# A two-layer trunk on one core: where the first loads are queued, where eight low parts are subtracted, and who writes the indexer's key a second time

## The chip, the core and the metric

The kernel runs on one core of one Trainium2 chip. The core has five engines, each with a queue of its own that it works through in order: TensorE (PE: matmuls, and PEld for the loads of their weights), VectorE (DVE), ScalarE (ACT), GpSimd (POOL) and SyncE (SP), which here only issues DMAs. 16 DMA engines move data between the chip's memory (HBM) and the core's SBUF. The metric is the device time of one execution in microseconds (us); a profile shows one execution.

## The reference

The trunk has two layers on 256 tokens of width 1024. Layer 0 is a sparse attention whose keys are chosen by an indexer, layer 1 a stick-breaking attention; each has a SiLU gate, an output projection and a layer norm of ALPHA * x + sublayer(x). What matters here is layer 0:

```python
q, k, v, g, qi, wi, ki = jnp.split(x @ w_in, cuts, axis=-1)
q = apply_rope(q.reshape(b, s, N_HEADS, HEAD_DIM), cos, sin)
k = apply_rope(k.reshape(b, s, N_HEADS, HEAD_DIM), cos, sin)
qi = apply_rope(qi.reshape(b, s, IDX_HEADS, IDX_DIM), cos, sin)
ki = apply_rope(ki[:, :, None, :], cos, sin)[:, :, 0, :]
...
rel = jax.nn.relu(jnp.einsum('bqhd,bsd->bqhs', qib, ki).astype(jnp.float32) * IDX_DIM ** -0.5)
score = jnp.einsum('bqhs,bqh->bqs', rel, wib)
...
_, idx = lax.top_k(score, k_top)
```

The 16 heads then attend to the 64 chosen keys (softmax), and `(o * silu(g)) @ w_out` goes into the layer norm. All is float32.

## The kernel before, in words

**Two parts for each number.** Every matmul of a projection works on a pair: a high part `wh` (the weight rounded to TensorE's float32r format, by ScalarE, L66) and a low part `wl` (the weight less its high part, by VectorE, L67). Three products are added: high by high, low activation by high weight, high activation by low weight. So one chunk is read by 8 matmuls of its `wh` and then by 4 of its `wl` (`tok_part`, L118); in the gates by 8 and 8 (L150, L152).

**Chunks.** All weights of both layers stand in HBM as 80 chunks of 128 x 1024 numbers, 512 KB each, in the order in which they are read. Layer 0's are q0 (chunks 0 to 3), k0 (4 to 7), v0 (8 to 11), k1 (12 to 15), q1 (16 to 19), v1 (20 to 23), eight gates (24 to 31) and the output projection (32 to 39). `fetch` loads a chunk into one of 4 `raw` buffers, through SP's queue, and splits it into one of 8 pairs of `wh` and `wl`. `load_chunk` keeps a few chunks ahead.

**The start.** Before the chunks come eight K tiles (`x_idx`): for each eighth of the width, 128 rows of the transposed x and of the indexer's weights, 420 KB. The first is loaded in three pieces; tiles 1 and 3 are issued from ScalarE's queue (L171), the others from SP's (L79). They take the same `raw` and `wh`/`wl` buffers. TensorE multiplies them in order (L231) into four banks `psi`.

**The indexer.** `rope` (L212 to L221) makes two products on VectorE (`ra`, `rb`) and adds them. For each of the two tiles of 128 tokens it is called for heads 0 to 4 and for heads 5 to 7 with the key, which is head 8; then GpSimd copies the key from place 8 to place 9 (L241), so that one transpose of places 8 and 9 (L275) gives the key twice, one copy for each half of the partitions. From the transposes come `zh`, `zl` (the key's parts) and `qih`, `qil` (L252, L253, in `select`), then scores (`rel` on ScalarE, `sc` on VectorE) and the choice of 64 keys by eight rounds of maximum and replacement for each token tile (L304, L305).

**Order.** `mix` interleaves the projections q0, k0, v0 with `select`; then a loop over the heads runs k1, q1, v1, the gates and the output projection beside the attention. On each engine a scheduler sets the order from this program, and the pools' free buffers set waits. Three banks (`pp`) hold projections: a block needs two, one for each token tile, so that k1's second token tile (L118) waits until ScalarE has copied v0's first tile out (`vt`, L357), and q1's second one until VectorE's rope of k1 has read its bank (`rb`, L219).

Of the kernel before, what the change touches and what calls it, by code (L numbers as in the profile page):

```python
# [9 lines left out]
F32 = mybir.dt.float32  # L10
F32R = mybir.dt.float32r
AF = mybir.ActivationFunctionType
OP = mybir.AluOpType

P = 128
# [5 lines left out]
HD = 64  # L21
# [7 lines left out]
CW = 1024  # L29
WARM = 6  # L30
AHEAD = 2
IDX_A = 5 * HD
IDX_W = IH * HD + HD + IH
NEG_ADM = -1.0e38
# [8 lines left out]
def trunk(ctx: ExitStack, tc: tile.TileContext, x_rows, x_idx, w_all, consts, lnp, out):  # L43
    nc = tc.nc

    def pool(name, bufs, **kw):
        return ctx.enter_context(tc.tile_pool(name=name, bufs=bufs, **kw))
# [5 lines left out]
    wraw = pool("wraw", 4)  # L53
    wspl = pool("wspl", 8)
# [5 lines left out]
    def as32(t):  # L60
        return t.bitcast(F32)
# [3 lines left out]
    def split(h, lo, src):  # L65
        copy = nc.scalar.activation(h, src, AF.Copy)  # L66
        nc.vector.tensor_sub(lo, src, as32(h))  # L67
        return copy
# [8 lines left out]
    def load(dst, src):  # L77

        tc.keep_in_program_order(nc.sync.dma_start(dst, src))  # L79

    ahead = []
    n_chunk = [0]

    def fetch():
        c = n_chunk[0]
        if c == w_all.shape[0]:
            return
        n_chunk[0] += 1
        raw = wraw.tile([P, CW], F32, name="raw", tag="raw")
        load(raw, w_all[c])  # L90
        wh = wspl.tile([P, CW], F32R, name="wh", tag="wh")
        wl = wspl.tile([P, CW], F32R, name="wl", tag="wl")
        split(wh, wl, raw)
        ahead.append((wh, wl))

    def load_chunk():
        while len(ahead) <= AHEAD:
            n = len(ahead)
            fetch()
            if len(ahead) == n:  # L100
                break
        return ahead.pop(0)

    def bank(p, w=512):
        return p.tile([P, 512], F32, name="bank", tag="bank")[:, :w]
# [59 lines left out]

    cuts = (slice(0, IDX_A), slice(IDX_A, IDX_W))
    idx_w = []
    for k in range(KT):
        raw = wraw.tile([P, CW], F32, name="raw", tag="raw")[:, :S + IDX_W]
        if k:  # L170
            (nc.scalar.dma_start if k in (1, 3) else load)(raw, x_idx[k])  # L171
        else:
            first = S + IDX_A
            load(raw[:, :S], x_idx[k, :, :S])
            nc.scalar.dma_start(raw[:, S:first], x_idx[k, :, S:first])
            load(raw[:, first:], x_idx[k, :, first:])
        wh = wspl.tile([P, CW], F32R, name="wh", tag="wh")[:, :IDX_W]
        wl = wspl.tile([P, CW], F32R, name="wl", tag="wl")[:, :IDX_W]
        if k:
            split(xTh[:, k], xTl[:, k], raw[:, :S])  # L180
        else:
            nc.vector.tensor_copy(xTh[:, k], raw[:, :S])
            nc.vector.tensor_sub(xTl[:, k], raw[:, :S], as32(xTh[:, k]))
        for c in cuts if k == 0 else (slice(0, IDX_W),):
            copy = split(wh[:, c], wl[:, c], raw[:, S + c.start:S + c.stop])
            if k == 0:
                tc.keep_in_program_order(copy)
        idx_w.append((wh, wl))

    fetch()  # L190
    cs = cst.tile([P, C_W], F32, name="cs")
    load(cs, consts)
# [18 lines left out]
        nc.gpsimd.memset(as32(zl), 0.0)  # L211
        zpad.append((zh, zl))  # L212

    def rope(dst, ps, heads, t):
        v = ps.rearrange("p (h d) -> p h d", d=HD)
        a = wk.tile([P, 8, HD], F32, name="ra", tag="ra")[:, :heads]
        b = wk.tile([P, 8, HD], F32, name="rb", tag="rb")[:, :heads]
        nc.vector.tensor_mul(a, v, cos[:, t, None, :].to_broadcast([P, heads, HD]))
        nc.vector.tensor_mul(b, v, sin[:, t, None, :].to_broadcast([P, heads, HD]))  # L219
        halves = [u.rearrange("p h (e d) -> p h e d", e=2) for u in (dst, a, b)]  # L220
        nc.vector.tensor_add(halves[0], halves[1], halves[2][:, :, ::-1, :])  # L221


    psi = [[bank(at) for _ in range(2)] for t in range(NT)]
    for k in range(KT):
        w = idx_w[k]
        for xp, wp in ((0, 0), (1, 0), (0, 1)):
            xk = (xTh, xTl)[xp]
            for t in range(NT):
                for n in range(2):  # L230
                    nc.tensor.matmul(psi[t][n][:, :cuts[n].stop - cuts[n].start],  # L231
                                     xk[:, k, t * P:(t + 1) * P], w[wp][:, cuts[n]],
                                     start=k + xp + wp == 0, stop=k == 7 and wp == 1)
    for _ in range(AHEAD):
        fetch()
    ri, wi = [], []
    for t in range(NT):
        r = sb.tile([P, D], F32, name=f"ri{t}", tag=f"x{t}")[:, :10 * HD].rearrange("p (h d) -> p h d", d=HD)
        rope(r[:, :5], psi[t][0][:, :IDX_A], 5, t)
        rope(r[:, 5:9], psi[t][1][:, :4 * HD], 4, t)  # L240
        nc.gpsimd.tensor_copy(r[:, 9], r[:, 8])  # L241
        w = few.tile([P, IH], F32, name=f"wi{t}")
        nc.vector.tensor_scalar(w, psi[t][1][:, 4 * HD:4 * HD + IH], float(np.float32(IH ** -0.5)), None,
                                op0=OP.mult)
        ri.append(r)
        wi.append(w)
# [304 lines left out]
    for t in range(NT):  # L551
        for n in range(2):
            if t == 0:
                wv[n] = list(load_block())
            ps = bank(pp)
# [160 lines left out]
```

## Time and profile before

| | |
|---|---|
| median of 3 runs | 309.99 us (309.28 to 310.41) |
| the profiled execution | 310.33 us, of which the span from the first to the last instruction is 308.4 us |
| TensorE busy | 296.5 us (96%) |
| VectorE, ScalarE, GpSimd busy | 245.1, 203.7, 9.0 us |
| chain that ended last | 83% TensorE, 7% VectorE, 5% DMA |
| read from HBM | 49.05 MB |

A busy TensorE includes matmuls that overlap their neighbours, so its share says when it stood, not how well it ran. Times in the rows below count from the start of the span. A row of the timeline gives start, duration, engine, line, operation, what is written from what, shapes and count; in brackets stands how long the engine was idle before and what ended that.

### The profile page before, as it was taken

What the parts mean: (1) busy time and instruction counts of PE and PEld (TensorE: products, weight loads), DVE (VectorE), ACT (ScalarE), POOL (GpSimd) and SP (SyncE); (2) the same over time, 40 slices, a digit from 0 to 9 for tenths busy, and PEclk for the clock granted to TensorE, in tenths of its full rate; (3) what the DMA queues carried; (4) which work ended last, traced back from release to release, by engine and by line L of the source; (5) the groups of instructions that cost most, each with busy time, mean ns of one, the idle gap of its engine ahead of it and who ended that gap; (6) DMA issues with size and microseconds to landing.
All of it is one profiled execution on the core that took longest, in us unless ns stands there. A gap on an engine that the chain in (4) does not pass through costs nothing.

```text
span 308.4 us, 4668 instructions
## 1 busy us (share of the span) xinstructions
PE 296.5 (96%) x1640; PEld 248.7 (81%) x1640; DVE 245.1 (79%) x517; ACT 203.7 (66%) x427; POOL 9.0 (3%) x18
## 2 busy tenths in 40 slices
PE   7998999999999999999999999999999999999990
PEld 4886888787888888878788888888888888877790
DVE  3669999899999687977499573886898999884385
ACT  4656673475569999998415374767599999985200
POOL 3011000000000000000010100000000000000011
PEclk9999999999999999999999999999999999999997
DMA  7796543876068854254424459785543353000003
GB/s 262 229 349 189 177 156 112 275 258 218 9 240 270 307 191 140 105 216 134 166 68 132 142 154 385 251 292 167 190 132 88 118 160 115 0 2 1 0 16 122
DMA packets 14567, 50.40 MB, mean 163 GB/s; under 512 B 1616, under 2 KB 2000, under 8 KB 14544
## 3 DMA queue, kind: packets, MB, share of 16 engines
q1 hardware_dynamic: 14112, 49.08, 48.5%
q10 hardware_dynamic: 432, 1.02, 0.9%
q8 instruction: 13, 0.21, 0.3%
q14 instruction: 10, 0.08, 0.1%
HBM read 49.05 MB, written 1.05 MB: 162 GB/s over the span
## 4 chain that ended last, share of the span: by engine, by line
PE 83%; DVE 7%; DMA 5%; ACT 1%; issue 1%; POOL 0%; DVEq 0%; SPq 0%; ACTq 0%
PE bank L118 36%; PE bank L150 19%; PE bank L152 10%; PE bank L372 3%; DVE wl L67 3%; DMA raw<-x_idx 3%; DMA raw<-w_all 2%; PE bank L141 1%; PE bank L373 1%; PE bank L605 1%; PE bank L142 1%; PE bank L143 1%; ACT wh L66 1%; DVE sc L305 1%; PE bank L584 1%
## 5 line engine op out<-in xcount | busy, mean ns | idle before, releaser
L66 ACT ACTIVATE wh<-raw 128x1024 fp32r<-128x1024 f32 (+2 forms) x89 | 90.0, 1017 | 52.0 <-DMA raw<-w_all 30.8
L67 DVE TENSOR_TENSOR wl<-raw,wh 128x1024 fp32r<-128x1024 f32 (+2 forms) x89 | 103.5, 1166 | 25.3 <-ACT wh L66 24.9
L118 PE MATMUL bank<-wh,xT 128*128 128x512 f32 x192 | 49.8, 395 | 1.4 <-ACT vt L357 0.7
L150 PE MATMUL bank<-yT,wh 128*128 128x512 f32 x192 | 48.6, 395 | 0.0
L118 PEld LDWEIGHTS bank<-wh,xT 128*128 128x128 f32 x192 | 35.3, 188 | 9.4 <-ACT vt L357 1.2
L150 PEld LDWEIGHTS bank<-yT,wh 128*128 128x128 f32 x192 | 34.5, 188 | 7.1 <-issue 0.3
L152 PEld LDWEIGHTS bank<-yT,wl 128*128 128x128 f32 x192 | 26.2, 190 | 1.9
L152 PE MATMUL bank<-yT,wl 128*128 128x256 f32 x192 | 26.7, 282 | 0.0
L118 PE MATMUL bank<-wl,xT 128*128 128x512 f32 x96 | 26.7, 390 | 0.0
L118 PEld LDWEIGHTS bank<-wl,xT 128*128 128x128 f32 x96 | 18.0, 188 | 3.9
L118 PE MATMUL bank<-wh,oh 128*128 128x512 f32 (+1 forms) x80 | 20.8, 355 | 0.0
L118 PE MATMUL bank<-wh,ol 128*128 128x512 f32 (+1 forms) x80 | 20.7, 350 | 0.0
L118 PE MATMUL bank<-wl,oh 128*128 128x512 f32 (+1 forms) x80 | 20.3, 349 | 0.0
L118 PE MATMUL bank<-wh,yT 128*128 128x512 f32 x64 | 17.4, 391 | 0.0
L150 PE MATMUL bank<-xT,wh 128*128 128x512 f32 x64 | 16.3, 396 | 0.0
L118 PEld LDWEIGHTS bank<-wh,ol 128*128 128x128 f32 x80 | 14.0, 189 | 2.1 <-issue 0.2
L118 PEld LDWEIGHTS bank<-wl,oh 128*128 128x128 f32 x80 | 14.0, 189 | 2.0 <-issue 0.2
L118 PEld LDWEIGHTS bank<-wh,oh 128*128 128x128 f32 x80 | 13.5, 189 | 2.3 <-issue 0.6
L428 ACT ACTIVATE p<-ml,mx 128x128 f32<-128x128 f32 (+1 forms) x32 | 14.2, 448 | 1.2 <-DVE mx L423 1.1
L155 DVE TENSOR_TENSOR bank<-bank,low 128x256 f32<-128x256 f32 x32 | 13.6, 424 | 0.7 <-ACT low L154 0.4
L118 PEld LDWEIGHTS bank<-wh,yT 128*128 128x128 f32 x64 | 11.9, 188 | 2.4
L150 PEld LDWEIGHTS bank<-xT,wh 128*128 128x128 f32 x64 | 11.7, 188 | 2.3
(138 smaller groups left out, 508.1 us busy)
## 6 DMA issues: line engine op xcount, KB each, us to landing
raw<-w_all SPq DMA_DIRECT2D x80, 512.0 KB, 4.2
raw<-x_idx SPq DMA_DIRECT2D x5, 420.0 KB, 4.2
gb<-lnp SPq DMA_DIRECT2D x4, 512.0 KB, 6.2
x<-x_rows SPq DMA_DIRECT2D x2, 512.0 KB, 4.4
y<-x SPq DMA_DIRECT2D x4, 256.0 KB, 2.0
raw<-x_idx ACTq DMA_DIRECT2D x2, 420.0 KB, 5.2
cs<-consts SPq DMA_DIRECT2D x1, 512.0 KB, 6.8
raw<-x_idx ACTq DMA_DIRECT2D x1, 160.0 KB, 2.7
```

The lines of the kernel that those rows point to most:

```text
L66: copy = nc.scalar.activation(h, src, AF.Copy)
L67: nc.vector.tensor_sub(lo, src, as32(h))
L118: nc.tensor.matmul(ps, src[kk][xp][:, t * P:(t + 1) * P], wc[wp][:, k, :], start=kk == 0 and xp + wp == 0, stop=kk == 7 and wp == 1)
L141: nc.tensor.matmul(ps, sh, mh, start=first, stop=False)
L142: nc.tensor.matmul(ps, sh, ml, start=False, stop=False)
L143: nc.tensor.matmul(ps, sl, mh, start=False, stop=last)
L150: nc.tensor.matmul(ps, wh[:, k, :], both[:, k], start=k == 0, stop=k == 7)
L152: nc.tensor.matmul(ps[:, :S], wl[:, k, :], high[:, k], start=False, stop=k == 7, skip_group_check=True)
L155: nc.vector.tensor_add(ps[:, :S], ps[:, :S], low)
L305: nc.vector.match_replace(out=sc, in_to_replace=m8, in_values=sc, imm_value=NEG_REP)
L372: nc.tensor.matmul(po[rs, n * S:(n + 1) * S], vt[0][:, hs], p0(i), start=True, stop=False)
L428: nc.scalar.activation(p[:, i, :], m[:, i, :], AF.Exp, bias=mx[:, c], scale=-1.0, accum_out=sm[:, c])
```

## The change

Three things change. All eight K tiles are issued from SP's queue, except the middle piece of the first. The indexer's key is written to places 8 and 9 by `rope` itself: its last add is split into one for the other heads and one that writes the key twice. And for chunks 6, 9, 12, 15, 18, 21, 24 and 27 (`DMA_LOW`), ScalarE writes the negated high part into `wl` and the high part into `wh`, and a DMA issued by GpSimd adds the chunk from HBM to `wl`, in place of VectorE's subtraction. Those chunks are begun up to two places earlier than they are read (`begin`), which also changes the order of SP's loads: 4, 6, 5, 7, 9, 8, 10, 12, 11 and so on.

```diff
+DMA_LOW = range(6, 30, 3)
...
+    begun = {}
+
+    def begin(c):
+        raw = wraw.tile([P, CW], F32, name="raw", tag="raw")
+        load(raw, w_all[c])
+        wh = wspl.tile([P, CW], F32R, name="wh", tag="wh")
+        wl = wspl.tile([P, CW], F32R, name="wl", tag="wl")
+        if c in DMA_LOW:
+            nc.scalar.activation(wl, raw, AF.Copy, scale=-1.0)
+            nc.scalar.activation(wh, raw, AF.Copy)
+            nc.gpsimd.dma_start(wl, w_all[c], accum_op=OP.add)
+        else:
+            split(wh, wl, raw)
+        begun[c] = wh, wl
...
-        raw = wraw.tile([P, CW], F32, name="raw", tag="raw")
-        load(raw, w_all[c])
-        wh = wspl.tile([P, CW], F32R, name="wh", tag="wh")
-        wl = wspl.tile([P, CW], F32R, name="wl", tag="wl")
-        split(wh, wl, raw)
-        ahead.append((wh, wl))
+        for n in range(c, c + 3):
+            if n not in begun and (n == c or n in DMA_LOW):
+                begin(n)
+        ahead.append(begun.pop(c))
...
-            (nc.scalar.dma_start if k in (1, 3) else load)(raw, x_idx[k])
+            load(raw, x_idx[k])
...
-        nc.vector.tensor_add(halves[0], halves[1], halves[2][:, :, ::-1, :])
+        one = heads - twice
+        nc.vector.tensor_add(halves[0][:, :one], halves[1][:, :one], halves[2][:, :one, ::-1, :])
+        if twice:
+            last = [u[:, one:].to_broadcast([P, 2, 2, HD // 2]) for u in (halves[1], halves[2][:, :, ::-1, :])]
+            nc.vector.tensor_add(halves[0][:, one:], *last)
...
-        rope(r[:, 5:9], psi[t][1][:, :4 * HD], 4, t)
-        nc.gpsimd.tensor_copy(r[:, 9], r[:, 8])
+        rope(r[:, 5:10], psi[t][1][:, :4 * HD], 4, t, twice=True)
```

The order of instructions moves with it. The names are the program's, with their buffers' numbers; line numbers differ between the two, since the changed kernel is 20 lines longer.

First place: ScalarE's row about the key's high part `zh0`, before (chunks 4, 5 and 6 stand ahead of it)

```order
L66 ACTIVATE wh_384<-raw_382 128x1024
L66 ACTIVATE wh_402<-raw_400 128x1024
L66 ACTIVATE wh_491<-raw_489 128x1024
L252 ACTIVATE zh0_177<-bank_406 64x256
L252 ACTIVATE qih_325<-bank_413 128x512
```

and now (chunk 4, then 6 with L95 and L94 about chunk 5).

```order
L68 ACTIVATE wh_384<-raw_382 128x1024
L95 ACTIVATE wh_390<-raw_388 128x1024
L68 ACTIVATE wh_409<-raw_407 128x1024
L94 ACTIVATE wl_391<-raw_388 128x1024
L272 ACTIVATE zh0_177<-bank_413 64x256
L272 ACTIVATE qih_325<-bank_420 128x512
```

One activation of 1024 columns more stands ahead of `zh0`, and chunk 5 comes after chunk 6.

Second place: VectorE's row up to k0's rope (`ra`, `rb`), before (the low part is that of chunk 9; three others stand between `zl` and this one)

```order
L67 TENSOR_TENSOR wl_578<-raw_575,wh_577 128x1024
L297 SCALAR_TENSOR_TENSOR sc0_469<-rel_585,wi0_309,sc0_469 128x128
L297 SCALAR_TENSOR_TENSOR sc1_470<-rel_593,wi1_323,sc1_470 128x256
L297 SCALAR_TENSOR_TENSOR sc0_469<-rel_585,wi0_309,sc0_469 128x128
L297 SCALAR_TENSOR_TENSOR sc1_470<-rel_593,wi1_323,sc1_470 128x256
L218 TENSOR_TENSOR ra_609<-bank_487,cs_167 128x512
```

and now (the low parts are those of chunks 8, 10, 11 and 13; that of 7 stands further ahead).

```order
L69 TENSOR_TENSOR wl_552<-raw_549,wh_551 128x1024
L317 SCALAR_TENSOR_TENSOR sc0_476<-rel_559,wi0_309,sc0_476 128x128
L69 TENSOR_TENSOR wl_632<-raw_629,wh_631 128x1024
L317 SCALAR_TENSOR_TENSOR sc0_476<-rel_559,wi0_309,sc0_476 128x128
L317 SCALAR_TENSOR_TENSOR sc1_477<-rel_567,wi1_323,sc1_477 128x256
L69 TENSOR_TENSOR wl_657<-raw_654,wh_656 128x1024
...
L69 TENSOR_TENSOR wl_699<-raw_696,wh_698 128x1024
L317 SCALAR_TENSOR_TENSOR sc1_477<-rel_595,wi1_323,sc1_477 128x256
L235 TENSOR_TENSOR ra_611<-bank_494,cs_167 128x512
```

Five low parts stand between `zl` and the rope now, and four before.

Third place: ScalarE's row up to the copies `vt0` and `vt1` of v0's two banks, before (chunks 12 to 15)

```order
L66 ACTIVATE wh_671<-raw_669 128x1024
L66 ACTIVATE wh_695<-raw_693 128x1024
L66 ACTIVATE wh_758<-raw_756 128x1024
L66 ACTIVATE wh_776<-raw_774 128x1024
L357 ACTIVATE vt0_345<-bank_625 128x512
L357 ACTIVATE vt1_346<-bank_626 128x512
```

and now (chunks 15, 14, 16, 18, 17 and 19).

```order
L94 ACTIVATE wl_705<-raw_702 128x1024
L95 ACTIVATE wh_704<-raw_702 128x1024
L68 ACTIVATE wh_768<-raw_766 128x1024
L68 ACTIVATE wh_798<-raw_796 128x1024
L95 ACTIVATE wh_804<-raw_802 128x1024
L94 ACTIVATE wl_805<-raw_802 128x1024
L68 ACTIVATE wh_823<-raw_821 128x1024
L68 ACTIVATE wh_872<-raw_870 128x1024
L377 ACTIVATE vt0_345<-bank_627 128x512
L377 ACTIVATE vt1_346<-bank_628 128x512
```

Four chunks more, up to 19, stand ahead of the copies.

## Rows read from the trace of the kernel before

**Rows 1.** Table of stretches: busy time and count by engine, clock, DMA.

```profile
core 0: us, PE busy (x) PEld busy (x) DVE busy (x) ACT busy (x) POOL busy (x), PEclk, DMA share, GB/s
0.00:19.00 19.00, 16.81 (x102) 14.08 (x102) 9.70 (x19) 10.02 (x18) 2.53 (x11) 1.00 0.79 271
19.00:38.00 19.00, 17.91 (x88) 14.76 (x87) 18.72 (x32) 12.16 (x15) 2.68 (x3) 1.00 0.66 215
38.00:60.00 22.00, 22.00 (x105) 18.29 (x104) 21.53 (x46) 9.45 (x16) 0.00 (x0) 1.00 0.53 165
60.00:77.00 17.00, 15.62 (x70) 12.28 (x69) 16.01 (x40) 11.34 (x15) 0.00 (x0) 1.00 0.77 251
77.00:160.00 83.00, 83.00 (x480) 69.36 (x479) 67.83 (x183) 65.69 (x175) 0.35 (x1) 1.00 0.51 172
...
288.00:308.40 20.40, 13.29 (x82) 11.81 (x80) 13.30 (x29) 0.75 (x2) 1.84 (x2) 0.92 0.14 52
```

**Rows 2.** TensorE's waits: for whom, us in total, times, longest.

```profile
PE bank L275 <- POOL ri L241: 1.1, 1, 1.1
PE bank L231 <- ACT wh L66: 0.9, 2, 0.6
PE bank L118 <- ACT vt L357: 0.7, 1, 0.7
PE bank L118 <- DVE rb L219: 0.7, 1, 0.7
```

**Rows 3.** Timeline of all engines, K tiles 1 to 3.

```profile
1.18 0.93 ACTq L171 DMA_DIRECT2D raw<-x_idx  x2
...
7.98 0.42 ACT L66 ACTIVATE xT<-raw 128x256 fp32r<-128x256 f32 x1 [1.86 <-DMA raw<-x_idx]
...
8.89 0.40 ACT L66 ACTIVATE xT<-raw 128x256 fp32r<-128x256 f32 x1
...
9.03 1.35 PE L231 MATMUL bank<-wh,xT 128*128 128x320 f32 x8 [0.60 <-ACT wh L66]
```

**Rows 4.** Timeline of all engines, the key and its copies.

```profile
25.15 0.24 POOL L241 COPY ri<-ri 128x64 f32<-128x64 f32 x1 [4.77 <-DVE ri L221]
...
26.98 0.43 DVE L221 TENSOR_TENSOR ri<-ra,rb 128x256 f32<-128x256 f32 x1
...
27.47 1.17 POOL L241 COPY ri<-ri 128x64 f32<-128x64 f32 x1 [2.08 <-DVE ri L221]
...
28.70 0.33 PE L275 MATMUL bank<-cs,ri 128*128 128x128 f32 x1 [1.09 <-POOL ri L241]
```

**Rows 5.** Timeline of VectorE: chunk 6, q0's rope, k1's rope.

```profile
35.84 1.22 DVE L67 TENSOR_TENSOR wl<-raw,wh 128x1024 fp32r<-128x1024 f32 x1
36.97 0.69 DVE L221 TENSOR_TENSOR rq<-ra,rb 128x512 f32<-128x512 f32 x1
...
75.43 0.67 DVE L219 TENSOR_TENSOR rb<-bank,cs 128x512 f32<-128x512 f32 x1
```

**Rows 6.** Timeline of TensorE: transposes of q0, low part of chunk 6.

```profile
38.23 0.82 PE L329 MATMUL bank<-cs,rq 128*128 128x128 f32 x6
...
43.83 1.07 PE L118 MATMUL bank<-wl,xT 128*128 128x512 f32 x4
```

**Rows 7.** Timeline of ScalarE: chunk 6, the key, chunk 15, `vt`.

```profile
28.90 1.06 ACT L66 ACTIVATE wh<-raw 128x1024 fp32r<-128x1024 f32 x1 [0.84 <-DMA raw<-w_all]
29.86 0.36 ACT L252 ACTIVATE zh<-bank 64x256 fp32r<-64x256 f32 x1
...
59.64 1.06 ACT L66 ACTIVATE wh<-raw 128x1024 fp32r<-128x1024 f32 x1 [1.56 <-PE bank L118]
60.61 1.07 ACT L357 ACTIVATE vt<-bank 128x512 f32<-128x512 f32 x2
```

**Rows 8.** Table of stretches, columns as in rows 1: chunks 6 to 24.

```profile
28.00:76.00 48.00, 46.17 (x218) 37.84 (x218) 46.44 (x98) 27.14 (x41) 0.64 (x1) 1.00 0.62 195
```

**Rows 9.** DMA issues: queue, count, KB each, median us to landing.

```profile
raw<-w_all SPq DMA_DIRECT2D x80, 512.0 KB, 4.2
```

More of the change, by code (lines that the diff above doesn't have):

```diff
@@ L212, in trunk, with rope @@
         zpad.append((zh, zl))
-    def rope(dst, ps, heads, t):
+    def rope(dst, ps, heads, t, twice=False):
         v = ps.rearrange("p (h d) -> p h d", d=HD)
```

## The prediction

> **What bounds the kernel now.** I read the table of stages first [rows 1]. TensorE is busy for all but 12 of 308.4 us, at a granted clock of 1.00 (the upper of its two levels, 2.4 GHz) everywhere but in the last stretch, so only its idle time can be won. The table says where that is: 19 - 16.81 = 2.2 us up to 19 us, 1.1 us from 19 to 38, 1.4 us from 60 to 77, and 7.1 us in the tail behind 288. From 38 to 60 and from 77 to 160 there is none, although ScalarE or VectorE is nearly full there; they are behind, but within the buffers. The view of TensorE's waits then names the four that an edit can reach [rows 2]: 0.9 us for the high parts of the K tiles, 1.1 us for GpSimd's copy of the indexer's key, 0.7 us for the `vt` copies that free v0's banks, 0.7 us for the rope of k1. They add up to 3.4 us. The low parts (`wl`) stand in no row of that view: no matmul waits for one directly, so taking eight of them off VectorE pays only through what stands behind them in VectorE's row. The tail belongs to the last layer norm, which the change doesn't touch.
>
> **K tiles.** ScalarE's queue issues tiles 1 and 3 at 1.18 us beside SP's loads [rows 3]. Tile 2 from SP lets ScalarE begin at 7.98, after 1.86 us of waiting; tile 3 is there at 8.89 without a wait, so the two came together, and TensorE stood 0.60 us before tile 2 at 9.03. In one queue tile 2 goes ahead of tile 3. Two tiles of 0.43 MB at the 271 GB/s of that stage [rows 1] take 3.2 us, one alone 1.6 us; so tile 2 can come up to 1.6 us sooner, and TensorE can use at most its 0.9 us of waits [rows 2], with about 0.1 us of refilling. Bounds: 0 (the tiles come no sooner) and 1.0; I take 0.8, near the upper end, since tile 2 needs to gain only half of what its order gives. The raw buffers come free earlier in step, so chunk 0, the tables and VectorE's row follow by 0.8 us.
>
> What the Trainium skill states under "Issuing engines are not separate DMA queues" (DMA: Bandwidth & Descriptors) speaks against a gain: all queues run on the same 16 engines and a second one saves only issue time. By that alone this term would be 0 and the forecast 308.7; the row agrees that bandwidth is shared, but what is won here is the order of arrival, not bandwidth.
>
> **Key written twice.** The copy on GpSimd took 0.24 us for the first token tile and 1.17 us for the second [rows 4]; TensorE's transposes began as it ended, at 28.70. Now VectorE writes the key itself: its last add of 256 columns (0.43 us) becomes one of 192 and one of 128. No row has these; an extra add costs between 0 and 0.43 us, and I take 0.2, as most of a short instruction is its start. Both token tiles stand before the second transpose, so 0.4 us. Saved at this place: 1.17 + 0.1 (hand-over) - 0.4, some 0.8 us.
>
> **What is late next.** VectorE is busy 18.72 of the 19 us up to 38 [rows 1], so TensorE, now 1.6 us ahead, runs into the rope of q0: its last add ran from 36.97 to 37.66 [rows 5], its transposes began at 38.23 [rows 6]. VectorE's row begins 0.8 us sooner and has 0.4 us more to do. And ScalarE's order has changed (the first place shown): chunk 6 is loaded before chunk 5, and its negated high part, 1.06 us, stands before `zh`. Before, the seventh chunk's activation began as it landed, at 28.90, and `zh` at 29.86 [rows 7]; now that load comes at 28.1, chunk 5 takes until 29.2, the negated part until 30.2, and `zh` comes 0.35 us later than before instead of 0.8 us sooner; VectorE's `zl` and `qil` behind it lose some 0.4 us. In all -0.8 + 0.4 + 0.4 = 0: the rope ends at 37.7 as before, and TensorE is at these transposes at 37.75. It has then done one more matmul of 512 columns than before at this place (two of L118 more, one of L143 less by the order; about 0.23 us). So 0.5 + 0.2 = 0.7 us is kept of the 1.6. Bounds: 0 and 1.6.
>
> Between 38 and 60 VectorE's order pulls chunks 10, 11 and 13 ahead of k0's rope, five low parts of 1.22 us instead of four (the second place). That rope frees the bank for v0's second token tile. By the order TensorE does 13 matmuls of the first tile before it asks, some 3 us; I put the loss at 0.2, between 0 and the 1.2 us of the low part.
>
> **v0's banks.** `vt` began at 60.61 because chunk 15's high part ran from 59.64 [rows 7]; TensorE waited 0.7 us [rows 2]. Now chunks 14 to 19 stand before `vt` (the third place). Each needs one of eight buffers: with 20 chunks begun, 12 must have been read, so the last one, chunk 19, starts when TensorE has read the high part of chunk 11, about 1 us before v0 ends, and takes 1.06 us: `vt` can start just as v0 ends. Gain 0.7 and 0.1 of refilling, 0.8; it is 0 if chunk 19's load is late by 1 us.
>
> **k1's rope.** It held TensorE for 0.7 us, with its `rb` running from 75.43 [rows 2, 5] and VectorE busy 16.01 of 17 us [rows 1]. The low parts of chunks 15 and 18 are gone there, those of 14, 16 and 17 moved ahead: over 2 us less in front of the rope. Gain 0.8, lower bound 0.
>
> **The accumulating DMAs.** Eight times VectorE's 1.22 us goes; ScalarE gets eight activations of 1.06 us, 8.5 us, in a stretch where it was busy 27.14 of 48 us [rows 8]; that hides them but for the one priced above. The DMA itself stands in no row. A plain load of a chunk takes 4.2 us from issue to landing [rows 9]. Chunk 6 has the least cover: negated part ready at 30.2, low part read at 43.83 less 0.7 [rows 6], 12.9 us; the others are begun earlier still. So from 4.2 up to 12.9 us its price is 0. In engine time a load costs 0.52 MB over 195/0.62 = 315 GB/s [rows 8], 1.7 us; six before 76 us add 10 to the 30 us in use, of 48. It fits at the rate of a load. Issuing on GpSimd delays nothing else: it has no other work between the key's copies and the layer norm, busy 0.64 us in all of that stretch [rows 8].
>
> **Sum.** -0.7 (start and key) + 0.2 (v0) - 0.8 - 0.8 = -2.1 us. The profiled execution took 310.33 us with a span of 308.4; the 1.9 us around it stay. That gives 308.2 for it, and from the median of 309.99, 307.9. Over 0.5%, 1.55 us, is about what can be told from no change.
>
> **Rivals.** (a) Nothing is handed back at q0's rope: `zh` isn't late, all 1.6 us are kept and v0 loses nothing: 0.8 + 0.8 + 1.6 = 3.2, so 306.8. For it: VectorE had 0.3 us idle and `zl` need not be next to late. Against it: 0.57 us between rope and transposes. (b) The gains further on don't come: accumulating DMAs share the engines with the loads, chunks 8, 13 and 19 land a us or two later, and ScalarE, which works in order, holds `rel` and `vt` behind them. Then 0.7 is kept at the start, v0 loses 1.0, and the last two gains shrink to 0.2 together: 310.1. For it: share 0.62 before the change [rows 8]. Against it: most chunks are begun 8 us or more ahead. (c) Slower: an accumulating DMA holds the engines for much longer than a load. The free engine time in 28 to 76 is 0.38 x 48 = 18 us; for six that is 3.0 us each, and this is the point from which loads fall behind. At 5 us each, 12 us are missing; the lead of the chunks, 6.8 us from the end of chunk 6's low part at 37.06 to its reading [rows 5, 6], covers the half, so 5.2 us of waiting less the 2.1 won: 313. Against it: nothing but the 1.7 us of a load.
>
> The Trainium skill has a rule beside (c): an add in the DMA engines reads two sources and so goes at half the rate (Collectives: The Full Stack, "The bandwidth ceiling: the fold count and why AG ≠ RS ≠ AR"). No row here shows it; with 1.7 us doubled each would hold the engines for 3.4 us, 6 x 0.4 = 2.4 us past the point and within the lead of the chunks, so it would be (b), 310.1, whose chance is given from rows.
>
> **How the numbers follow.** Forecast 0.46, with a range of its own from 307.0 to 309.0; (a) 0.17, (b) 0.24, (c) 0.13. Faster by over 0.5%: (a) and most of the forecast, 0.57; within: the rest of it and most of (b), 0.30; slower 0.13. The range of 8 in 10 goes from 305.8, all of [rows 2] won with refilling, to 310.8, past (b); (c) stays outside.
>
> **What would show it.** TensorE's waits for GpSimd, `vt` and `rb` gone from the view; a new one at q0's transposes (L349) for `rq`, up to 1 us; third K tile on TensorE near 8.2. Wrong: any matmul that waits for the DMA of a `wl`, loads landing in 6 us or more, ScalarE idle before `rel` or `vt`, or a longer time outside the span.

## The result, and the profile after

The changed kernel took 318.49 us (median of 6 runs, 317.38 to 320.83) beside 310.25 us for the kernel before (309.28 to 310.97): ratio 1.0264, 95% interval 1.0228 to 1.0300. It is slower by 8.2 us, where 307.9 us was forecast. The profiled execution took 317.54 us with a span of 315.4; before it was 310.33 and 308.4, so 7.0 us of it lie inside the span. Medians in this document leave out one execution of 320.24 us, of the kernel called "every second full" below, which was in a slower state of the chip.

The table of stretches of the kernel after, with the columns of [rows 1]:

```profile
core 0: us, PE busy (x) PEld busy (x) DVE busy (x) ACT busy (x) POOL busy (x), PEclk, DMA share, GB/s
0.00:19.00 19.00, 16.95 (x104) 14.52 (x105) 10.68 (x20) 10.12 (x18) 3.05 (x12) 1.00 0.84 274
19.00:38.00 19.00, 17.86 (x86) 14.24 (x84) 17.98 (x33) 12.50 (x15) 1.40 (x2) 1.00 0.76 252
38.00:60.00 22.00, 19.45 (x90) 15.95 (x91) 17.41 (x37) 13.99 (x22) 2.59 (x3) 1.00 0.97 252
60.00:77.00 17.00, 13.99 (x58) 11.04 (x57) 13.51 (x41) 10.31 (x14) 1.73 (x2) 0.90 1.00 270
77.00:100.00 23.00, 22.02 (x109) 17.88 (x108) 20.42 (x53) 16.02 (x36) 1.73 (x2) 1.00 0.93 270
```

VectorE got the room that was meant for it: 17.41 us instead of 21.53 from 38 to 60, 13.51 instead of 16.01 from 60 to 77. TensorE lost there all the same, 22.00 to 19.45 and 15.62 to 13.99. The column that moved most is the share of the DMA engines, 0.53 to 0.97 and 0.77 to 1.00. TensorE's waits in the kernel after (us in total, times, longest), to be laid beside [rows 2]:

```profile
PE bank L134 <- DVE rb L236: 3.5, 3, 1.5
PE bank L134 <- ACT vt L377: 3.0, 1, 3.0
PE bank L179 <- DVE rest L176: 1.2, 1, 1.2
PE bank L157 <- ACT rel L314: 1.2, 1, 1.2
PE bank L252 <- ACT wh L68: 0.9, 2, 0.7
```

The wait for GpSimd is gone, but `rb` went from 0.7 to 3.5, `vt` from 0.7 to 3.0, and `rel` is new. L179 is the 1.2 us that TensorE waits at the start for the zeros of its first matmuls (`rest`); every kernel of this case has it, some under another line number. Without it these are 8.6 us against the 3.4 us of [rows 2]: 5.2 of the 7.0 us. The rest is in the clock. This is the table of stretches around the wait for `vt`:

```profile
62.00:66.60 4.60, 1.66 (x9) 1.02 (x7) 1.64 (x4) 2.61 (x5) 0.86 (x1) 0.98 0.93 287
66.60:68.00 1.40, 1.33 (x3) 1.14 (x4) 1.30 (x6) 0.76 (x3) 0.00 (x0) 0.50 0.96 190
68.00:70.00 2.00, 2.00 (x6) 1.53 (x6) 1.96 (x7) 1.20 (x2) 0.00 (x0) 0.55 1.04 231
70.00:72.00 2.00, 2.00 (x10) 1.60 (x10) 1.94 (x9) 1.30 (x2) 0.38 (x1) 1.00 1.00 391
```

When TensorE began again it was granted 0.50, the lower level of 1.2 GHz, then 0.55 up to 70: 1.4 x 0.5 + 2.0 x 0.45 = 1.6 us more. 5.2 + 1.6 = 6.8 of 7.0 us.

No matmul waits for the DMA of a `wl`. Here is who is late instead, in the timelines of ScalarE, VectorE and TensorE after:

```profile
49.84 1.06 ACT L68 ACTIVATE wh<-raw 128x1024 fp32r<-128x1024 f32 x1 [1.92 <-DMA raw<-w_all]
...
64.06 2.07 ACT L68 ACTIVATE wh<-raw 128x1024 fp32r<-128x1024 f32 x2 [1.99 <-DMA raw<-w_all]
66.04 1.07 ACT L377 ACTIVATE vt<-bank 128x512 f32<-128x512 f32 x2
```

```profile
50.94 1.22 DVE L69 TENSOR_TENSOR wl<-raw,wh 128x1024 fp32r<-128x1024 f32 x1 [0.99 <-ACT wh L68]
...
53.47 0.68 DVE L236 TENSOR_TENSOR rb<-bank,cs 128x512 f32<-128x512 f32 x1
```

```profile
54.30 1.16 PE L134 MATMUL bank<-wh,xT 128*128 128x512 f32 x4 [1.53 <-DVE rb L236]
...
66.67 2.07 PE L134 MATMUL bank<-wh,xT 128*128 128x512 f32 x4 [3.01 <-ACT vt L377]
```

TensorE was done with v0's first bank by 62.4, and `vt` could have begun then; it stands in ScalarE's row behind two high parts, those of chunks 17 and 19, and each began as its load landed. By the trace chunk 17's load was issued at 55.77 and landed at 63.98, 8.2 us later; chunk 19's landed at 64.99, after 6.8 us. At 50.94 it is VectorE's row: a low part waits for its high part, that for its load, and the rope of k0 stands behind. The loads and the accumulating DMAs of the kernel after, by line, with the time from issue to landing (the loads from 28 to 92 us):

```profile
L81 SPq DMA_DIRECT2D raw<-w_all x23: 327/328/482, 28.3 to 88.6; - x23
...
DMA to landing us min/median/max: 3.5/5.7/10.3
```

```profile
L96 POOL DMA_DIRECT2D wl<-w_all x8: 862/865/1025, 30.6 to 92.5; - x8
...
DMA to landing us min/median/max: 7.6/9.0/10.7
```

and the loads of the kernel before in that stretch:

```profile
L79 SPq DMA_DIRECT2D raw<-w_all x21: 327/328/542, 28.6 to 90.0; - x21
DMA to landing us min/median/max: 3.4/4.3/4.9
```

So each accumulating DMA landed within the cover that it had, but loads that had taken 4.9 us at most took up to 10.3.

### The profile page after: what moved, and what is told of

It is laid out like the page before. It is cut to its first block, busy times and chain, and to the rows that moved or that the text cites. A ratio compares the mean times of both kernels' runs of the same rounds, so it can differ in the third digit from the quotient of the medians.

```text
span 315.4 us, 4711 instructions
## 1 busy us (share of the span) xinstructions
PE 298.4 (95%) x1640; PEld 250.2 (79%) x1640; DVE 239.2 (76%) x511; ACT 211.1 (67%) x435; POOL 14.3 (5%) x24
## 4 chain that ended last, share of the span: by engine, by line
PE 72%; DMA 12%; DVE 9%; ACT 3%; issue 2%; SPq 0%; DVEq 0%; ACTq 0%
PE bank L134 28%; PE bank L166 19%; DMA raw<-w_all 10%; PE bank L168 10%; PE bank L392 3%; DVE wl L69 3%; DMA raw<-x_idx 2%; DVE sc L325 1%; PE bank L393 1%; DVE m L324 1%; PE bank L625 1%; ACT wh L68 1%; PE bank L157 1%; PE bank L604 1%; PE bank L603 1%
## 5 line engine op out<-in xcount | busy, mean ns | idle before, releaser
L69 DVE TENSOR_TENSOR wl<-raw,wh 128x1024 fp32r<-128x1024 f32 (+2 forms) x81 | 93.6, 1160 | 29.6 <-ACT wh L68 29.3
L68 ACT ACTIVATE wh<-raw 128x1024 fp32r<-128x1024 f32 (+2 forms) x81 | 81.4, 1011 | 44.9 <-PE bank L134 16.9
L134 PE MATMUL bank<-wh,xT 128*128 128x512 f32 x192 | 51.4, 401 | 6.5 <-DVE rb L236 3.5
```

Source lines behind the costliest of these rows:

```text
L134: nc.tensor.matmul(ps, src[kk][xp][:, t * P:(t + 1) * P], wc[wp][:, k, :], start=kk == 0 and xp + wp == 0, stop=kk == 7 and wp == 1)
```

## The experiments

The theory at the start (A): the accumulating DMAs hold the DMA engines and make the loads late, and late loads hold `rel`, `vt` and the ropes in the in-order rows of ScalarE and VectorE. Rivals: the changed order of instructions by itself (B), the small parts (C), ScalarE's eight activations more (D). The last column of this table is the sum of TensorE's waits in the one execution that was profiled, without L179; landings are of loads issued from 28 to 92 us. Each ratio is to executions of the kernel before that were timed beside that kernel (their medians lie from 310.05 to 310.35 us).

| kernel | median us | ratio to before, 95% | landing, median / longest | waits |
|---|---|---|---|---|
| before | 310.25 | | 4.3 / 4.9 | 3.4 |
| after | 318.49 | 1.0264 (1.0228-1.0300) | 5.7 / 10.3 | 8.6 |
| small parts alone | 309.29 | 0.9978 (0.9945-1.0010) | 4.3 / 5.2 | 2.7 |
| order, VectorE subtracts | 308.82 | 0.9956 (0.9923-0.9990) | 4.4 / 5.8 | 1.8 |
| VectorE adds | 309.60 | 0.9985 (0.9952-1.0018) | 4.5 / 5.9 | 4.2 |
| plain copies | 313.77 | 1.0108 (1.0067-1.0150) | 5.2 / 7.7 | 6.4 |
| 8 columns added | 311.42 | 1.0046 (1.0025-1.0066) | 4.4 / 6.3 | 4.5 |
| added from the raw tile | 325.32 | 1.053 (1.046-1.060) | 4.7 / 9.4 | 14.8 |
| eight in layer 1 | 312.69 | 1.0092 (1.0062-1.0122) | | 4.6 |
| four only | 318.59 | 1.0271 (1.0237-1.0304) | 5.2 / 8.7 | 8.8 |
| 512 columns added | 314.94 | 1.0149 (1.0078-1.0220) | 5.0 / 8.6 | 7.3 |
| every second full | 315.29 | 1.0181 (1.0122-1.0240) | 5.5 / 10.6 | 8.7 |
| first three full | 316.20 | 1.0188 (1.0159-1.0218) | 4.4 / 9.6 | 6.3 |
| GpSimd subtracts | 321.03 | 1.0349 (1.0323-1.0375) | 4.2 / 5.7 | 10.5 |
| after, six raw buffers | 309.39 | 0.9982 (0.9963-1.0000) | 8.2 / 11.5 | 3.6 |
| small parts, six raw | 307.03 | 0.9904 (0.9884-0.9924) | 4.4 / 6.6 | 2.6 |
| order, six raw | 306.48 | 0.9884 (0.9861-0.9907) | 4.5 / 7.5 | 2.6 |
| order again | 308.68 | 0.9956 (0.9941-0.9971) | 4.4 / 5.1 | 2.3 |
| before, six raw | 308.56 | 0.9923 (0.9892-0.9954) | 4.8 / 6.0 | 2.1 |
| order, eight raw | 305.73 | 0.9841 (0.9810-0.9872) | 4.9 / 8.0 | 1.2 |

### The small parts, the order, ScalarE's work and the traffic

Small parts alone:

```diff
-DMA_LOW = range(6, 30, 3)
+DMA_LOW = ()
```

> The changed kernel with no low part made by a DMA: K tiles in one queue and the key written twice by its rope are all that is left of the change. Theory A (the accumulating DMAs and their traffic make the chunks late): with them gone the loss goes too, and the start gains about what TensorE waited less there; 308.5 to 310 against 310.25 before. Theory B (the changed order of instructions, chunks begun ahead of their turn, makes the loss): the same, 308.5 to 310, since the order is back too. Rival C (the two small parts lose something themselves, as the K tiles' new order or one more add in front of the rope of q0): slower than before, 311 or more.

The order without DMAs:

```diff
-            nc.scalar.activation(wl, raw, AF.Copy, scale=-1.0)
-            nc.scalar.activation(wh, raw, AF.Copy)
-            nc.gpsimd.dma_start(wl, w_all[c], accum_op=OP.add)
+            split(wh, wl, raw)
```

> The changed kernel with its chunks begun in the changed order (6 before 5, 9 before 8 and so on), but every low part subtracted by VectorE as before; no accumulating DMA, no negated part on ScalarE. Theory A (the DMAs): the order alone costs little, 308.5 to 312, with loads landing in about 4 us. Theory B (the order): the most of the loss stays, 315 to 319.

VectorE adds:

```diff
-            nc.gpsimd.dma_start(wl, w_all[c], accum_op=OP.add)
+            nc.vector.tensor_add(wl, raw, as32(wl))
```

> The changed kernel with the same activations on ScalarE, the negated high part too (eight more of 1.06 us), but the weights are added to it by VectorE from the raw tile and not by a DMA. Theory A (the DMAs): 309 to 313, ScalarE's 8.5 us more and VectorE's 9.8 us given back cost little between them. Rival D (ScalarE's eight activations more hold rel and vt up): 315 to 319 without any accumulating DMA.

Plain copies:

```diff
-            nc.gpsimd.dma_start(wl, w_all[c], accum_op=OP.add)
+            nc.gpsimd.dma_start(wl, w_all[c])
```

> The changed kernel instruction for instruction, with the eight DMAs of GpSimd not accumulating: each writes the chunk's weights over the negated part (so the product with the low part is wrong, and the output is not the reference's). The same bytes are read from HBM by the same queue at the same places. Theory A1 (the adding itself holds the DMA engines): packets of this queue take about 0.2 us as those of a load do, against 0.345 us, and the time falls to 310 to 313. Theory A2 (the queue of GpSimd, its casting or the second reading of the weights does it, adding or not): 316 to 319, with packets of 0.3 us or more.

Measured: 309.29, 308.82, 309.60 and 313.77 us. C and D fall, and B in its plain form: the small parts, the order of chunks and ScalarE's activations together cost nothing that shows. Three kernels without these DMAs are within 0.8 us of each other. Plain copies, in the order of the change, took 4.2 us more than adding on VectorE, whose order differs at some places, and making them add cost another 4.7 in one and the same order. 313.77 lies between the ranges of A1 and A2, and neither was right alone: the traffic costs and the adding costs.

How the two queues share the DMA engines can be counted from the packets of the trace (those of 4096 bytes; how many started in that microsecond on the 16 engines, and the mean time of one):

```
kernel, us           loads (SP's queue)      GpSimd's queue
after, 51 to 52       82 packets, 0.193 us    none
after, 54 to 55       35 packets, 0.173 us    31 adding, 0.327 us
after, 55 to 56       37 packets, 0.173 us    35 adding, 0.327 us
plain copies, 36-37   52 packets, 0.171 us    45 plain,  0.173 us
layer 1, 196 to 197   31 packets, 0.175 us    35 adding, 0.338 us
```

Where both queues have work, about as many packets of the one start as of the other. An adding one takes nearly twice as long, so a load beside it gets little more than a third of the engines' time: its 128 packets need 128/35 = 3.7 us instead of 128/82 = 1.6. Over the whole profile an adding packet took 0.345 us on average and a plain one from the same queue 0.192. The Trainium skill states the sharing (DMA: Bandwidth & Descriptors, "Queues, rings and completion order": an engine goes round between the queues that have work, packet by packet), and the trace agrees with 35 to 31 and 37 to 35 per us. The Trainium skill's half rate for an add, weighed in the prediction (Collectives: The Full Stack, which states it for a reduce-scatter), agrees nearly: 0.345/0.192 = 1.8.

### How much of it is traffic, and whether it is in proportion

Eight columns:

```diff
-            nc.gpsimd.dma_start(wl, w_all[c], accum_op=OP.add)
+            nc.gpsimd.dma_start(wl[:, :8], w_all[c, :, :8], accum_op=OP.add)
```

> The changed kernel with the same order of instructions on TensorE, VectorE and ScalarE, but each of the eight DMAs adds only the first 8 of 1024 columns (the other columns of those low parts stay negated, so the output is not the reference's). The traffic of the DMAs is gone, the order that the scheduler laid around them is not. Theory A (the traffic makes the loads late, and that is all): 309 to 310.5, as where VectorE adds (309.60), with loads landing in 4 to 5 us. Theory B2 (the order that the scheduler lays when low parts are left to a DMA costs by itself: chunks' activations ahead of vt, low parts ahead of the ropes): the 4.2 us by which the plain copies exceeded 309.60 stay, 312.5 to 314, with TensorE waiting for rb and vt although loads are on time.

From the raw tile:

```diff
-            nc.gpsimd.dma_start(wl, w_all[c], accum_op=OP.add)
+            nc.gpsimd.dma_start(wl, raw, accum_op=OP.add)
```

> The changed kernel with the eight DMAs adding from the raw tile in SBUF and not from HBM: the weights are read from HBM once, the adding stays; a raw buffer is held until its DMA has read it, and the order differs at some places. Theory A1 (the DMA engines' time for the adding is what counts): packets of about 0.34 us as before, and 313 to 318. Rival (reading the weights twice from HBM is what counts): loads land in 4 to 5 us again, and 309 to 312.

In layer 1, `DMA_LOW = range(56, 80, 3)`:

> Eight low parts by accumulating DMAs as in the change, but of chunks 56, 59 to 77 of layer 1, where DMA engines were busy for 0.45 of the time; layer 0 as without any. This shows the price of one undisturbed. Theory A1 (adding is slow in itself): packets of 0.3 us or more also there, landing in 6 to 9 us, and no loss beside the kernel without them (309.3), 308.5 to 310.5, since there is room. Rival (0.345 us is queueing at engines that are full): packets of 0.2 us and landings of 4 to 6 us.

Four only, `DMA_LOW = range(6, 30, 6)`:

> Only every second one of the eight: low parts of chunks 6, 12, 18 and 24 by accumulating DMAs. Theory A (DMA engines full from 38 to 92 us): with half of it the engines have room (about 0.85 instead of 0.97 to 1.00), and the loss is nearly gone, 309.5 to 312. Rival (each such DMA costs by itself, wherever there is room): half of the 9.2 us between 309.3 and 318.5, so 313 to 315.

With 8 columns 311.42 us, the order of the change at every instruction of TensorE, VectorE and ScalarE: about 1.8 us of the loss lie in that order or in the eight small DMAs themselves (309.60 where VectorE adds), the other 7.1 in the traffic. The time lies between the ranges of A and B2; B2 named a part of it, 2 of 9 us. Since the order is the same, this kernel also tells which of the waits are the traffic's. Its waits, L179 left out:

```profile
PE bank L134 <- DVE rb L236: 1.9, 2, 1.0
PE bank L252 <- ACT wh L68: 1.3, 1, 1.3
PE bank L157 <- ACT rel L314: 0.7, 1, 0.7
PE bank L295 <- DVE ri L242: 0.6, 1, 0.6
```

L252 is the K tiles, L295 the key. By the trace the two waits for `rb` are those of q0's rope (0.91 us) and of k1's (1.03), which the changed kernel has too (1.01 and 0.97): they belong to the order. The wait for k0's rope (1.53) and that for `vt` (3.01) are gone, that for `rel` fell from 1.15 to 0.67, and the clock stayed at 1.00 from 60 to 70. These three, 5.0 us together, and the 1.6 us of the clock are what the traffic cost in the profiled executions.

Adding from the raw tile, without a second reading of HBM, has packets of 0.328 us: what is slow is the adding, not HBM. But it took 325.32 us. The raw buffer is held until its DMA has read it, and the next load waits for the buffer; the chain that ended last contains this DMA with 5%. I had not expected that loss; it is the first sign that buffers decide, and not engine time alone.

In layer 1 the packets took 0.353 us at a share of 0.36 to 0.80, so 0.345 is the price of one and not a queue at full engines. The loss of 3.4 us beside 309.29 was not expected there; the profile shows a new wait for `sg` of 1.3 us, the rest I did not trace.

Four of them lost as much as eight, 318.59 us. Both numbers written down were wrong. Its order differs from that of the change; this is ScalarE's row in it, then VectorE's:

```profile
75.78 1.06 ACT L95 ACTIVATE wh<-raw 128x1024 fp32r<-128x1024 f32 x1 [1.55 <-DMA raw<-w_all]
76.86 0.38 ACT L272 ACTIVATE zh<-bank 64x256 fp32r<-64x256 f32 x1
```

```profile
77.27 0.43 DVE L273 TENSOR_TENSOR zl<-bank,zh 64x256 fp32r<-64x256 f32 x1 [1.16 <-ACT zh L272]
...
78.29 0.69 DVE L236 TENSOR_TENSOR rb<-bank,cs 128x512 f32<-128x512 f32 x1
```

A load issued at 70.11 landed at 75.68; `zh`, `zl` and the rope of k1 stand behind it, one after the other, and TensorE waited 2.9 us for `rb` and then had a clock of 0.50 from 81 to 83. From 81 to 85 the DMA engines did nothing (share 0.00): the next load was issued only at 85.36, 11 us after the last.

### The same order, less traffic; and the adding on GpSimd itself

512 columns: as with 8, with `:512`.

> The changed kernel in the same order of instructions; each of the eight DMAs adds 512 of the 1024 columns (the other half of those low parts stays negated, so the output is not the reference's). With 8 columns it took 311.4 us, with 1024 318.5. Theory A (the loss follows the DMA engines' time, here about half of 2.75 us each): 314 to 315.5. Rival T (nothing is lost until the engines are full): 311 to 313. Rival N (each such DMA costs for being one, whatever its size): 317 or more.

Every second full:

```diff
-            nc.gpsimd.dma_start(wl, w_all[c], accum_op=OP.add)
+            nc.gpsimd.dma_start(wl[:, :8 + 1016 * (c % 6 == 0)], w_all[c, :, :8 + 1016 * (c % 6 == 0)], accum_op=OP.add)
```

> The changed kernel in the same order of instructions; the DMAs of chunks 6, 12, 18 and 24 add all columns, those of 9, 15, 21 and 27 only 8 (the rest of those low parts stays negated, so the output is not the reference's). Theory A (the loss follows the DMA engines' time): 314 to 316, half way between 311.4 and 318.5. Rival O (four are enough, as in the kernel with only these four, 318.6, since one late chunk at the wrong place in ScalarE's row holds everything): 317 to 319; the loss of that kernel came then not from its own order.

First three full: the same with `(c < 15)`.

> The changed kernel in the same order of instructions; the DMAs of chunks 6, 9 and 12 add all columns, the later five only 8 (the rest of those low parts stays negated, so the output is not the reference's). Theory A: only the waits up to about 56 us are left (the rope of k0 behind the low part of a late chunk), vt and the rope of k1 are on time; 312.5 to 314.5, and the transposes of k0 come as late as with all eight (62.4 us, against 59.5 before). Rival: vt is late all the same (because of ScalarE's order), 315 or more.

GpSimd subtracts:

```diff
-            nc.scalar.activation(wl, raw, AF.Copy, scale=-1.0)
             nc.scalar.activation(wh, raw, AF.Copy)
-            nc.gpsimd.dma_start(wl, w_all[c], accum_op=OP.add)
+            nc.gpsimd.tensor_sub(wl, raw, as32(wh))
```

> The low parts of the same eight chunks are taken from VectorE without any DMA: GpSimd, else idle, subtracts the rounded from the raw tile itself; ScalarE's eight activations more are gone too. If the intent of the change was sound and only its means too dear: 307.5 to 309, below the kernel with the two small parts alone (309.3), with a subtraction of 2 to 5 us on GpSimd. Rival (GpSimd's subtraction is long, or slows VectorE while it runs, as the key's second copy took 1.17 us where the first took 0.24): 311 or more.

In one and the same order the engine time of these DMAs (packets x mean / 16) and the time were: 8 columns 2 us, 311.42; three full 9, 316.20; every second 12, 315.29; half of the columns 12, 314.94; plain copies 12, 313.77; all adding 22, 318.49. It goes up from 2 to 22, but among the four in between the one with the least engine time is the slowest, and the executions of a single kernel lie as far apart as these four do (313.29 to 317.45 with half of the columns). A was right for half of the columns and for every second one; three full lie above its 314.5. There TensorE waited 3.7 us for the rope of k0, longer than with all eight (1.5), and k0's first transposes came at 66.29, where A had said 62.4; for `vt` it did not wait, as A had said and against the rival. With every second one TensorE waited 5.2 us at once for `rel`. Which instruction is caught behind a late load changes from kernel to kernel, and both of these long waits were followed by a clock of 0.50 for some 4 us (42.3 to 46 and 55.6 to 60) and of 0.71 to 0.78 for two more.

GpSimd's own subtraction is no way out. A row of GpSimd, then of VectorE:

```profile
36.75 2.87 POOL L95 TENSOR_TENSOR wl<-raw,wh 128x1024 fp32r<-128x1024 f32 x1 [7.21 <-DVE ra L234]
```

```profile
37.87 2.83 DVE L69 TENSOR_TENSOR wl<-raw,wh 128x1024 fp32r<-128x1024 f32 x1
41.49 1.21 DVE L69 TENSOR_TENSOR wl<-raw,wh 128x1024 fp32r<-128x1024 f32 x1
```

While GpSimd subtracts, VectorE's subtraction takes 2.83 us instead of 1.21, and up to 3.41 elsewhere; TensorE then waits 8.1 us for `rb`. The Trainium skill has this (SBUF — State Buffer, "Who interferes with whom": an operation of VectorE with two inputs in SBUF contends with one of GpSimd that reads SBUF, and the later one blocks).

### More lead for the loads

Two raw buffers more, for one pair of `wh` and `wl` less:

```diff
-    wraw = pool("wraw", 4)
-    wspl = pool("wspl", 8)
+    wraw = pool("wraw", 6)
+    wspl = pool("wspl", 7)
```

In the changed kernel:

> The changed kernel with all eight accumulating DMAs, six raw buffers instead of four and seven pairs of wh and wl instead of eight (the room for it): each load can be issued two chunks, some 5 us, sooner. Theory L (a load that meets an accumulating DMA comes 3 to 5 us late, and with four raw buffers nothing is loaded far enough ahead to hide that; late loads then hold rel, vt and the ropes in the rows of ScalarE and VectorE): most of the loss goes, 311 to 314. Rival (what is lost is lost in the order of ScalarE's and VectorE's rows, or the engines are simply full): 316 to 320.

In that of the small parts alone:

> The control to the one with six raw buffers: the two small parts of the change without any accumulating DMA, six raw buffers and seven pairs. By itself that should be worth nothing or little, since loads were mostly on time: 308 to 310 (309.3 with four and eight); above 311 if the eighth pair is missed.

In that of the order without DMAs:

> The changed order of chunks with VectorE subtracting all low parts (308.8 with four raw buffers), and six raw buffers and seven pairs. A candidate for the fastest: 308 to 309.5 if loads ahead help its two waits for the ropes (0.8 us each), above 310 if the eighth pair is missed.

The order without DMAs, with four, again:

> The kernel with the changed order of chunks and no DMA or ScalarE work more (308.8 us before, ratio 0.9956), once more, to see whether it beats the kernel before beyond doubt: ratio 0.994 to 0.998.

The changed kernel with all eight DMAs takes 309.39 us, 9.1 us less than with four raw buffers and below the 311 of theory L. Without the DMAs the same step brings 2.3 us (309.29 to 307.03), so some 6.8 us of the DMAs' loss are back. These are its loads from 28 to 92 us, and TensorE's waits:

```profile
L81 SPq DMA_DIRECT2D raw<-w_all x22: 327/328/453, 28.0 to 87.0; - x22
...
DMA to landing us min/median/max: 3.5/8.2/11.5
```

```profile
PE bank L157 <- ACT rel L314: 1.9, 1, 1.9
PE bank L134 <- DVE rb L236: 1.4, 1, 1.4
PE bank L179 <- DVE rest L176: 1.2, 1, 1.2
PE bank L134 <- DVE sg L416: 0.3, 1, 0.3
```

This is its table of stretches from 38 to 77, with the columns of [rows 1]:

```profile
38.00:60.00 22.00, 22.00 (x103) 17.96 (x104) 20.87 (x50) 15.04 (x22) 3.46 (x4) 1.00 0.96 281
60.00:77.00 17.00, 15.63 (x73) 12.51 (x72) 16.52 (x48) 8.47 (x13) 0.86 (x1) 1.00 0.92 271
```

The loads land later than ever, 8.2 us in the median, and the DMA engines are nearly as full (share 0.96 and 0.92, where the changed kernel had 0.97 and 1.00), but they are issued earlier, and TensorE waits 3.6 us instead of 8.6, at a clock of 1.00 in every stretch up to 288. Chunk 17's load, which held `vt`, shows it: by the trace it is now issued at 44.68 instead of 55.77, takes 9.8 us, and has landed 4.7 us before its high part begins at 59.15. It was not full engines that cost, then, but a landing time that grew beyond the lead of four buffers. The buffers change the order too (for 53 of VectorE's 511 instructions and 39 of ScalarE's 435; chunk 19's high part now stands behind `vt`), so this run doesn't part lead from order to the last us. Beside its control (307.03) the DMAs still cost 2.4 us.

Buffers alone in the kernel before, and eight raw buffers with six pairs in the order without DMAs:

> The kernel before with nothing changed but the buffers: six raw, seven pairs of wh and wl. Parts the gain of the fastest kernel (306.5) into that of the buffers and that of the rest. If the buffers alone bring it: 307 to 308.5, and what the small parts and the order add is 0.5 to 1.5 us; rival: with the K tiles on two queues the further raw buffers bring little, 309.5 or more.

> The changed order with VectorE subtracting all low parts, eight raw buffers and six pairs: two more of the same step that brought 308.7 to 306.5. If lead of the loads were still short: 305.5 to 306.3. If the pairs become what is short (a chunk's activation has to wait until TensorE has read an older pair): 307 or more.

Measured: 308.56 and 305.73 us. Two raw buffers more are worth 1.8 us to the kernel before (ratio 0.9923). The small parts and the order on top of them (0.9884), and then eight buffers (0.9841), are each 0.4% further by the ratios, 1.2 and 1.3 us, but at each of these two steps the intervals overlap, so neither is shown by itself. Less had been expected: the kernels with six raw buffers and no DMAs, 307.03 and 306.48 us, came out below their ranges. 305.73 us, ratio 0.9841 (0.9810 to 0.9872), beats both kernels: it has the K tiles in one queue, the key written twice, the new order of chunks, every low part on VectorE, and eight raw buffers.

## Why the prediction was wrong, point by point

Milestones of TensorE from the traces, us from the start of the span:

```
                             before   after    small parts alone
first transpose of the key    27.33    26.93    26.89
last transpose of the key     29.62    28.09    28.26
q0, first transposes          35.91    35.86    35.56
k0, first transposes          59.45    62.36    58.98
k1, first transposes         100.49   107.57    99.98
end of the last matmul       301.29   308.30   300.22
```

**K tiles**: 0.8 forecast, 0.4 at the first transpose of the key. That is one execution, and other kernels with the same K tile loads and four raw buffers have this transpose at 26.54 to 27.56, so the size of the gain is not measured; the wait for the K tiles' high parts stayed at 0.9 us. The third tile stood on TensorE at 8.82, not at 8.2. Tile 1, issued behind tile 0 instead of beside it, landed at 5.96 instead of 5.10, and TensorE waited 0.69 us for it at 7.03. The Trainium skill's rule beside this term pointed the right way: part of what the order of arrival won for tile 2, tile 1 lost.

**Key written twice**: 0.8 forecast; 1.5 us were won at the last transpose, less the 0.4 of the K tiles, so 1.1. Together 1.5, against 1.6.

**What is late next**: 0.7 forecast to be kept. With the small parts alone 0.5 was kept at k0 and 1.1 at the end. The rows were forecast rightly: `zh` began at 30.15 (30.2 forecast), and q0's rope ended at 37.77 (37.7). But in the changed kernel nothing was left at q0's first transposes (35.91 to 35.86), and the rope of q0 showed as a wait for `rb` of 1.0 us at 34.39, not for `rq` at L349. The wait for `rel` at 39.02 (1.15 us) wasn't in the sum.

**v0's second token tile**: a loss of 0.2 (up to 1.2) forecast; 1.5 us. **v0's banks**: a gain of 0.8 forecast, to be 0 if chunk 19's load was late by 1 us. That load took 6.8 us and chunk 17's before it 8.2, where 4.2 was the plain price, and `vt` cost 2.3 us more than before: the lower bound of 0 left no room for a loss. **k1's rope**: a gain of 0.8 forecast; the wait went from 0.67 to 0.97 us. That is not the DMAs' doing, since with 8 columns it is 1.03 and with the small parts alone 0.82: fewer low parts ahead of this rope did not bring it sooner, and what holds it there stays open. **The clock**: 1.6 us, in no term.

**The accumulating DMAs** are the step that failed. Their own cover was judged rightly: 9.0 us to landing lies between 4.2 and 12.9, and no matmul waited for one. Wrong was "It fits at the rate of a load". First the size: 22.1 us of engine time for eight (7.0% of 315.4), 2.76 each, not 1.7. Then the measure, which weighs more: the sum over 48 us against the free 0.38 says nothing of what a load meets while one runs. 2.76 us lies below the 3.0 us that I gave as the point from which loads fall behind, and they fell behind; plain copies, at 1.5 us each, already lost 2.4 us in the same order (313.77 beside 311.42). What the runs showed in its place is a landing time: 5.7 us in the median and 10.3 at most, where 4.3 and 4.9 had been, which four raw buffers did not hide; with six the landings were longer still and TensorE's waits 3.6 us. And the lead that I counted, 6.8 us from a low part's end to its reading, was that of the chunk, while what waits is `rel`, `vt` or a rope directly behind the chunk's activation in an in-order row, which had none: already in the kernel before ScalarE waited 26 times for a chunk to land, 30.8 us in all. In the changed kernel these waits are fewer, 17 and 21.5 us, so it is not their sum that costs but what stands behind the late ones.

Of the rivals, the mechanism of (b) is what happened, loads late and `rel` and `vt` held behind them, but its 310.1 let most of the gains go and put a loss of only 1.0 us beside them, at v0; (c) had the right sign with a point too high. Two of the signs named for being wrong came: loads in 6 us or more, ScalarE idle before `vt`. Two readings of the prediction were off without weight for the result: from 77 to 160 VectorE and ScalarE were busy 67.83 and 65.69 of 83 us, which is not nearly full, and all of [rows 2] with four times 0.1 us of refilling is 3.8 us, which gives 306.2 and not 305.8 as the lower end.

## What to carry to other kernels

Traffic that is added to busy DMA engines is to be priced by what it does to the landing time of the loads, against the lead that the buffers give them, and not by free engine time averaged over a stretch. Look in the rows of the in-order engines for what stands right behind an instruction that begins as its load lands: that has no cover, whatever the lead of the data itself. Before moving work off an engine, try two buffers more for the loads: here this alone was worth 1.8 us, and the moved work lost 8.2.

## What the runs showed of the hardware

- An accumulating DMA's packets of 4096 bytes took 0.328 to 0.353 us on average in seven kernels, from HBM or from SBUF, at full and at half-empty engines; plain ones from the same queue took 0.192. With 2048 bytes it was 0.184: nearly in proportion to the bytes.
- Two queues share a DMA engine packet for packet, not byte for byte: beside plain packets of 4096 bytes (37 from 55 to 56 us in the changed kernel, 45 from 82 to 83 us with 512 columns) there started 35 adding ones of 4096 bytes, and 54 of 2048. The queue with the slower packets gets the larger part of the engine.
- From GpSimd's issue to the first packet up to 5.0 us passed (30.56 to 35.61); for loads from SP's queue with no other DMA under way, in the kernel before, 0.95 to 1.00 us.
- After waits of 3.0 us (the changed kernel) and of 5.2 and 3.7 us (every second, first three) TensorE had 0.50 of its clock when it began again, for 3 to 4 us. After waits of 2.4 us it had 1.00 in the kernel with plain copies, but 0.64 and then 0.51 in the one with 512 columns.
